# A diagonal state-space (S5) mixer on 32-column tiles of the array, with its short convolution as Toeplitz products read back from memory, inside a two-block network kernel

## The chip, the cores and the metric

One core of one Trainium2 chip runs one program. The metric is device time in microseconds (us), the median of several executions. TensorE is called PE, VectorE DVE, ScalarE ACT, GpSimd POOL; SP issues most transfers (DMAs).

## What is computed

The reference runs two blocks over 256 tokens of width 1024: an attention and expert block, then a block of two layers with four feed-forward networks (FFN 0 to 3), an S5 mixer between FFN 0 and 1, and an attention mixer. The change concerns the S5 mixer and FFN 0 ahead of it:

```python
u = (h @ w_in)                      # 256 x 1024, 64 groups of 16 channels
def step(carry, u_c):               # per chunk of time, per group: 64 complex states
    bu = einsum('bcgn,gpn->bcgp', u_c, bb)
    pr, pi, sr, si = lax.associative_scan(combine, (lam_re_b, lam_im_b, bu_re, bu_im), axis=1)
    ...
    y = einsum('bcgp,gnp->bcgn', st_re, c_re) - einsum('bcgp,gnp->bcgn', st_im, c_im)
y = y + d_skip * u
g = gelu(y)
g = g * sigmoid(g @ w_glu)
out = g @ w_out
```

## The kernel before

Everything is f32; matrix products split each factor into a rounded part and a rest (`wh`, `wl` of the weights, `xh`, `xl` of the activations) and add three products. Weights come in units of 512 KB in the order of use (`Stream`): SP loads `raw`, ACT rounds it to `wh` (L74), DVE subtracts to get `wl` (L75). FFN 0 has eight `raw` buffers, the mixer four, and two pairs `wh`, `wl`. A scheduler orders the instructions of each engine. Inside `manual_schedule`, PE and DVE follow the program text.

The mixer cuts the 256 tokens into 32 chunks of 8. Its parts, by the names in the code:

- `u_tile(f)`, f = 0 to 7: 24 products (L317 to L319, `s5ups`) and a scaling on DVE into `uT` (L1170).
- the gather: `uT` is written to `u_dram`, and after f = 3 and f = 7 read back in another layout as `us` (8 transfers of 512 runs of 128 bytes each).
- `contribution(hf)`, two halves: 64 narrow products (`s5eps`, 128 instructions, since an f32 product is two passes) give what each chunk adds to the states; ACT copies it to `s5e`.
- `chunks(hf)`: the recurrence over the chunks on DVE, in two blocks of 16 chunks side by side, then a correction of the second block. The two halves run by turns where both can.
- `taps(f)`: the part of y from inside a chunk, 8 products over weights that POOL and ACT spread by `tap_weights` (`s5kb`).
- `spread` and `states_out(qt)`: the states are put on a block diagonal (`s5sbd`), multiplied (`s5sps`), and go through `y_dram` to `yt` in four quarters.
- the sum, GELU, split, and the GLU: eight tiles of 24 products (`s5gps`) with a sigmoid each; then the output projection.

The part between the last u_tile and the GLU stands in this order in the text:

```python
contribution(0); taps(0); taps(1); run(45)
contribution(1); run(99, 24); spread(0); run(0, 99); spread(1)
taps(2) ... taps(5); states_out(0); taps(6); states_out(1); states_in(0)
taps(7); states_out(2); states_in(1); states_out(3); states_in(2); states_in(3)
```

Of the kernel before, what the change touches and what calls it, by code (L numbers as in the profile page):

```python
# [21 lines left out]
P = 128  # L22
D = 1024
S = 256
# [103 lines left out]
class Net:  # L128
# [4 lines left out]
    def __init__(self, ctx, tc, i, out, tap=None):  # L133
# [18 lines left out]
        self.v_order = [*range(self.NLO, P), *range(self.NLO)]  # L152
        self.ada_late = list(range(5, 5 + 8 * 5, 5))
# [158 lines left out]
    def mode_a(self, ps, w, xh, xl):  # L312

        wh, wl = w
        for k in range(KT):
# [564 lines left out]
    def ffn(self, l, last_deep=None, out=None):  # L880
        nc, tc = self.nc, self.tc
        with tc.tile_pool(name=f"ffn{l}", bufs=2) as fp:
# [5 lines left out]
            prev = row = None  # L888
            for c in range(NFF):
                if c == last_deep:  # L890
                    self.stream.shallow()
# [66 lines left out]
    def s5_prep(self, lo, hi):  # L958
# [169 lines left out]
        self.s5 = (lam, cw, me, kr, grp, pr, pi)  # L1128

    def s5_mixer(self):  # L1130
        nc, tc, i = self.nc, self.tc, self.i
        Q = 32
        lam, cw, me, kr, grp, pr, pi = self.s5
        with ExitStack() as st:
            wp = st.enter_context(tc.tile_pool(name="s5w", bufs=1))
            dp = st.enter_context(tc.tile_pool(name="s5d", bufs=1, space=bass.MemoryType.DRAM))
            u_dram = dp.tile([64, 16, 8, Q], F32, name="u_dram")
            y_dram = dp.tile([64, 16, 8, Q], F32, name="y_dram")
            xh, xl = self.gained(self.cols[:, self.MIX_G : self.MIX_G + KT])
            rx = self.rstd()  # L1140
            row = None
            l8 = wp.tile([P, 2, 2, Q], F32, name="s5l8")
# [4 lines left out]
            kbs = {}  # L1147

            uT = wp.tile([P, KT, 8, Q], F32, tag="sA", name="s5uT")
            us = wp.tile([P, 64, Q], F32, tag="sB", name="s5us")  # L1150
            def tap_weights(f):
                kb = wp.tile([P, 8, 8, 16], F32, tag="s5kb", name="s5kb", bufs=5)
                k = kr[:, f].rearrange("p (k n) -> p k n", n=16)
                if f % 2:
                    for g in range(8):
                        nc.scalar.activation(kb[:, :, g], k, AF.Copy, scale=grp[:, g : g + 1])
                else:
                    nc.gpsimd.tensor_mul(kb, k.unsqueeze(2).to_broadcast([P, 8, 8, 16]),
                                         grp[:, 0:8].unsqueeze(1).unsqueeze(3).to_broadcast([P, 8, 8, 16]))
                kbs[f] = kb  # L1160

            for f in (0, 2):
                tap_weights(f)
            def u_tile(f):
                nonlocal row
                ps = self.pm.tile([P, S], F32, tag="m", name="s5ups")
                self.mode_a(ps, self.stream.next(), xh, xl)
                if row is None:
                    row = self.rstd_row(wp, rx)
                nc.vector.tensor_mul(uT[:, f], ps.rearrange("p (c s) -> p s c", s=8),  # L1170
                                     row.rearrange("p (c s) -> p s c", s=8))
                nc.sync.dma_start(u_dram[8 * f : 8 * f + 8].rearrange("g n s c -> (g n) (s c)"),
                                  uT[:, f].rearrange("p s c -> p (s c)"))
                if f % 4 == 3:
                    gs = slice(8 * f - 24, 8 * f + 8)
                    for s in range(8):
                        nc.sync.dma_start(us[16 * s : 16 * s + 16, gs], u_dram[gs, :, s].rearrange("g n c -> n g c"))

            yc = wp.tile([P, KT, S], F32, name="s5yc")
# [3 lines left out]

            def taps(f):

                kb = kbs.pop(f)
                ps = self.pm.tile([P, S], F32, tag="m", name="s5yps")
                for k in range(8):
                    nc.tensor.matmul(ps[:, k * Q :], kb[:, k].rearrange("p a b -> p (a b)"),
                                     uT[:, f, 0 : 8 - k].rearrange("p s c -> p (s c)"), start=(k == 0), stop=(k == 7))  # L1190
                nc.scalar.activation(yc[:, f], ps, AF.Copy)

            def contribution(hf):

                for b in range(2):
                    ps = self.pa.tile([P, 2, 8, Q], F32, tag=f"acc{2 * hf + b}", name="s5eps")
                    for q8 in range(8):
                        q = 16 * hf + 8 * b + q8
                        for half in range(2):
                            hs = slice(64 * half, 64 * half + 64)  # L1200
                            for r in range(2):
                                nc.tensor.matmul(ps[hs, r, q8], me[q // 8][:, q % 8, r, hs], us[:, 2 * q + half], start=True, stop=True,
                                                 tile_position=(0, 64 * half))
                    nc.scalar.activation(ee[hf][:, :, :, 8 * b : 8 * b + 8].rearrange("p c r q -> p r q c"), ps, AF.Copy)

            def chunks(hf):
# [3 lines left out]
                s4 = ss[hf].rearrange("p (b c) r q -> p b c r q", b=2)  # L1210
                e4 = ee[hf].rearrange("p (b c) r q -> p b c r q", b=2)
                bl = lambda a: a.unsqueeze(1).to_broadcast([P, 2, 2, 16])
                yield v.memset(s4[:, :, 0], 0.0)
                for c in range(16):
                    n = 2 if c < 15 else 1
                    t = wp.tile([P, 2, 2, 2, 16], F32, tag=f"s5t{hf}", name="s5t")
                    t0, t1 = t[:, 0, :n], t[:, 1, :n]
                    if c < 15:
                        yield v.tensor_mul(t0, bl(l8[:, 0, :, qs]), s4[:, :, c])
                        yield v.tensor_mul(t1, bl(l8[:, 1, :, qs]), s4[:, :, c, ::-1])  # L1220
                        yield v.tensor_add(t0, t0, e4[:, :, c])
                        yield v.tensor_add(s4[:, :, c + 1], t0, t1)
                    else:
                        t0, t1, end = t0[:, 0], t1[:, 0], s4[:, 1, 0]
                        yield v.tensor_mul(t0, l8[:, 0, :, qs], s4[:, 0, c])
                        yield v.tensor_mul(t1, l8[:, 1, :, qs], s4[:, 0, c, ::-1])
                        yield v.tensor_add(t0, t0, e4[:, 0, c])
                        yield v.tensor_add(end, t0, t1)
                sh = [P, 15, 2, 16]
                x = wp.tile([P, 2, 15, 2, 16], F32, tag="sB", name="s5x")  # L1230
                x0, x1 = x[:, 0], x[:, 1]
                yield v.tensor_mul(x0, pr[:, :, qs].unsqueeze(2).to_broadcast(sh), end.unsqueeze(1).to_broadcast(sh))
                yield v.tensor_mul(x1, pi[:, :, :, qs], end[:, ::-1].unsqueeze(1).to_broadcast(sh))
                yield v.tensor_add(s4[:, 1, 1:], s4[:, 1, 1:], x0)
                yield v.tensor_add(s4[:, 1, 1:], s4[:, 1, 1:], x1)

            yt = None
            sbd = []
            for hf in range(2):
                sb = self.xt_pool.tile([P, 2, 16, 2, Q], F32, tag=("xh", "xl")[hf], name="s5sbd")  # L1240
                nc.gpsimd.memset(sb, 0.0)
                sbd.append(sb)

            def spread(hf):
                for half in range(2):
                    hs = slice(64 * half, 64 * half + 64)
                    src = ss[hf][hs].rearrange("p c r q -> p r q c")
                    if hf and half:
                        nc.vector.tensor_copy(sbd[hf][hs, :, :, half], src)
                    else:  # L1250
                        nc.scalar.activation(sbd[hf][hs, :, :, half], src, AF.Copy)

            ys = []

            def states_out(qt):

                ps = self.pa.tile([P, 8, 2, Q], F32, tag=f"acc{qt}", name="s5sps")
                for j in range(8):
                    for r in range(2):
                        nc.tensor.matmul(ps[:, j], cw[qt][:, r, j, 1:9].rearrange("p a b -> p (a b)"),  # L1260
                                         sbd[qt // 2][:, r, 8 * (qt % 2) + j], start=(r == 0), stop=(r == 1))
                if qt % 2 == 0:
                    ys.append(wp.tile([P, 2, 8, 2, Q], F32, tag=f"sE{qt // 2}", name="s5ys"))
                yb = ys[qt // 2][:, qt % 2]
                nc.scalar.activation(yb, ps, AF.Copy)
                for s in range(8):
                    q = nc.sync if s < 5 else nc.gpsimd
                    q.dma_start(y_dram[16 * qt : 16 * qt + 16, :, s].rearrange("g n c -> n g c"),
                                yb[16 * s : 16 * s + 16].rearrange("p q h c -> p (q h) c"))

            def states_in(qt):
                nc.sync.dma_start(yt[:, 2 * qt : 2 * qt + 2],
                                  y_dram[16 * qt : 16 * qt + 16].rearrange("(f g) n s c -> (g n) f (s c)", f=2))
# [3 lines left out]
            def run(n0, n1=0):  # L1277

                while n0 > 0 or n1 > 0:
                    if n0 > 0:  # L1280
                        next(rec0, None)
                    if n1 > 0:
                        next(rec1, None)
# [332 lines left out]
```

## Time and profile before

| what | value |
| --- | --- |
| median of 3 runs (lowest to highest) | 2130.15 us (2126.07 to 2134.4) |
| the profiled execution: time, span of its core | 2132.57 us, 2130.8 us |
| mean granted clock of PE, share of full speed | 0.981 |
| busy: PE, DVE, ACT, POOL | 94%, 74%, 50%, 25% |
| mean DMA rate | 178 GB/s |

A busy PE is one with an instruction in its pipeline, so 94% is not 94% of its peak. Shares are over the whole span; the mixer is some 147 us of it and has its own limits.

### The profile page before, as it was taken

How to read it: one execution, taken by the hardware profiler on the slowest of the kernel's cores; microseconds unless marked ns; L12 is line 12 of the kernel's file. 1: busy time of each engine (PE TensorE's matmuls, PEld its weight loads, DVE VectorE, ACT ScalarE, POOL GpSimd, SP SyncE). 2: the span in 40 equal slices, each digit the busy share in tenths (PEclk: the TensorE clock that was granted, in tenths of full speed). 3: DMA queues.
4: the chain of work that ended last, by engine and by line, in shares of the span. 5: the costliest groups of instructions: out<-in, count | busy, mean ns of one | idle time of the engine just before them, and what ended most of it. 6: DMA issues, size and time to landing. Idle time of an engine off the chain costs nothing. (4 is left out here: it accounts for less than half of the span.)

```text
span 2130.8 us, 33013 instructions
## 1 busy us (share of the span) xinstructions
PE 2010.9 (94%) x11862; PEld 1742.7 (82%) x11862; DVE 1572.3 (74%) x2984; ACT 1071.8 (50%) x1785; POOL 540.9 (25%) x548
## 2 busy tenths in 40 slices
PE   6888899999999899999999997889999999899999
PEld 4667899999999677788878887878887888677887
DVE  7987489887889666998866667476667666776666
ACT  5663544443444444545555544455555555555554
POOL 2342003036999332000031112101111111210111
PEclk9999999999999999999999999899999999999999
DMA  9763355554444777555555536355554555444552
GB/s 340 252 223 109 119 186 171 179 173 153 159 149 152 259 249 243 174 182 180 186 175 189 188 130 148 81 178 175 188 189 161 188 187 188 144 141 143 189 189 97
DMA packets 129557, 378.54 MB, mean 178 GB/s; under 512 B 26897, under 2 KB 41281, under 8 KB 129266
## 3 DMA queue, kind: packets, MB, share of 16 engines
q1 hardware_dynamic: 128160, 372.71, 52.5%
q0 software_dynamic: 1232, 3.73, 0.6%
q8 instruction: 93, 1.52, 0.3%
q14 instruction: 70, 0.57, 0.1%
q10 hardware_dynamic: 2, 0.00, 0.0%
HBM read 366.95 MB, written 9.44 MB: 177 GB/s over the span
## 5 line engine op out<-in xcount | busy, mean ns | idle before, releaser
L75 DVE TENSOR_TENSOR wl<-raw,wh 128x1024 fp32r<-128x1024 f32 (+1 forms) x595 | 761.4, 1282 | 366.8 <-ACT wh L74 363.2
L74 ACT ACTIVATE wh<-raw 128x1024 fp32r<-128x1024 f32 (+1 forms) x628 | 662.3, 1056 | 564.5 <-issue 317.1
L906 POOL TENSOR_TENSOR sgl<-sgl,rrow 128x256 f32<-128x256 f32 x88 | 126.2, 1434 | 719.7 <-ACT sgl L905 719.7
L317 PE MATMUL ups<-xh,wh 128*128 128x256 f32 x1024 | 294.1, 287 | 0.3 <-ACT act_lo L761 0.3
L319 PE MATMUL ups<-xh,wl 128*128 128x256 f32 x1024 | 290.5, 284 | 0.0
L318 PE MATMUL ups<-xl,wh 128*128 128x256 f32 x1024 | 290.3, 284 | 0.0
L327 PE MATMUL gps<-xx,wh 128*128 128x512 f32 x704 | 256.2, 401 | 6.6 <-DVE xx L306 6.6
L327 PE MATMUL upps<-xx,wh 128*128 128x512 f32 x704 | 251.8, 396 | 0.0
L335 PE MATMUL acc<-wh,gl 128*128 128x512 f32 x512 | 203.1, 399 | 8.1 <-DVE gl L250 8.1
L333 PE MATMUL acc<-wh,gh 128*128 128x512 f32 x512 | 203.6, 399 | 3.0 <-ACT gh L249 2.8
L685 POOL TENSOR_SCALAR ob<-iota,idxT 128x128 f32<-128x128 f32 x256 | 194.8, 781 | 36.0 <-PE ups L319 32.3
L328 PE MATMUL gps<-xx,wl 128*128 128x256 f32 x704 | 199.5, 283 | 0.6 <-DVE wl L75 0.6
L328 PE MATMUL upps<-xx,wl 128*128 128x256 f32 x704 | 198.4, 282 | 0.0
L317 PEld LDWEIGHTS ups<-xh,wh 128*128 128x128 f32 x1024 | 194.6, 190 | 0.8 <-ACT act_lo L761 0.7
L318 PEld LDWEIGHTS ups<-xl,wh 128*128 128x128 f32 x1024 | 194.6, 190 | 0.1
L319 PEld LDWEIGHTS ups<-xh,wl 128*128 128x128 f32 x1024 | 194.5, 190 | 0.1
L327 PEld LDWEIGHTS gps<-xx,wh 128*128 128x128 f32 x704 | 134.1, 190 | 38.6 <-DVE xx L306 7.8
L327 PEld LDWEIGHTS upps<-xx,wh 128*128 128x128 f32 x704 | 132.2, 188 | 31.2
L334 PE MATMUL acc<-wl,gh 128*128 128x512 f32 x380 | 151.3, 398 | 0.8 <-DVE wl L75 0.8
L333 PE MATMUL acc<-wh,hh 128*128 128x512 f32 x352 | 139.2, 396 | 6.7 <-ACT hh L249 6.5
L328 PEld LDWEIGHTS gps<-xx,wl 128*128 128x128 f32 x704 | 134.5, 191 | 4.5 <-DVE wl L75 0.9
L334 PE MATMUL acc<-wl,hh 128*128 128x512 f32 x352 | 137.9, 392 | 0.0
(403 smaller groups left out, 3779.6 us busy)
## 6 DMA issues: line engine op xcount, KB each, us to landing
raw<-peer_u SPq DMA_DIRECT2D x128, 512.0 KB, 3.3
raw<-peer_v SPq DMA_DIRECT2D x128, 512.0 KB, 3.4
raw<-ffn_gate SPq DMA_DIRECT2D x88, 512.0 KB, 3.6
raw<-ffn_up SPq DMA_DIRECT2D x88, 512.0 KB, 3.3
raw<-ffn_down SPq DMA_DIRECT2D x88, 512.0 KB, 3.4
raw<-w_ada SPq DMA_DIRECT2D x48, 512.0 KB, 5.6
raw<-w_in SPq DMA_DIRECT2D x24, 512.0 KB, 4.8
raw<-moba_w_qkv SPq DMA_DIRECT2D x24, 512.0 KB, 3.5
```

What stands on the lines that cost most here:

```text
L74: nc.scalar.activation(h[:, :n], raw[:, :n], AF.Copy)
L75: nc.vector.tensor_sub(lo[:, :n], raw[:, :n], h[:, :n].bitcast(F32))
L317: self.nc.tensor.matmul(ps, wh[:, s], xh[:, k], start=(k == 0), stop=False)
L318: self.nc.tensor.matmul(ps, wh[:, s], xl[:, k], start=False, stop=False)
L319: self.nc.tensor.matmul(ps, wl[:, s], xh[:, k], start=False, stop=(k == KT - 1))
L327: self.nc.tensor.matmul(ps, wh[:, s], xx[:, k], start=(k == 0), stop=False)
L328: self.nc.tensor.matmul(ps[:, 0], wl[:, s], xx[:, k, 0], start=False, stop=(k == KT - 1))
L333: mm(acc, lh, wh, start=start, stop=False)
L334: mm(acc, lh, wl, start=False, stop=False)
L335: mm(acc, ll, wh, start=False, stop=stop)
L685: nc.gpsimd.tensor_scalar(b, iota, idx[:, 1, n : n + 1], None, ALU.is_equal)
L906: nc.gpsimd.tensor_mul(sg, sg, row)
```

## The change

Four things change together. First, `u_tile` gets its weight columns in another order, so `uT` can be gathered from SBUF to SBUF with runs of 128, 384 or 512 bytes, without `u_dram`, in three pieces (f 0 to 3, 4 to 6, 7; of the last piece ACT issues half). Second, the taps become a Toeplitz matrix of 128 x 128 per group. FFN 0 writes it to DRAM (`toeplitz_out`: per f one transfer of zeros and eight of 16 rows of blocks), and the mixer reads half of it (2 MB) at a time into `s5tt`. Third, `taps` and `states_out` use 32 columns of the array per product (`tile_position`), with chunks in the rows of the result and both added in the same PSUM bank; no block diagonal, no `y_dram`: DVE transposes in blocks of 32 instead. Fourth, the recurrence runs in four blocks of 8 chunks, a sweep over the block ends and a correction, first half 0, then half 1.

```diff
+    def toeplitz_out(self, zero):
+        nc, kr = self.nc, self.s5[-1]
+        nc.gpsimd.memset(zero, 0.0)
+        for f in range(KT):
+            nc.sync.dma_start(self.toep[:, f].rearrange("p g k -> p (g k)"), zero)
+            for s in range(8):
+                nc.sync.dma_start(self.toep[16 * s : 16 * s + 16, f, :, 16 * s :].rearrange("n g k -> g n k"),
+                                    kr[:, f, : P - 16 * s])
...
             for c in range(NFF):
+                if 1 < c < NFF - 2:
+                    next(beside, None)
+                    next(beside, None)
...
+            def load_taps(hf):
+                toeplitz[hf] = wp.tile([P, 4, 8, P], F32, tag="s5tt", name="s5tt")
+                for f in range(4):
+                    nc.sync.dma_start(toeplitz[hf][:, f], self.toep[:, 4 * hf + f])
...
-            for f in (0, 2):
-                tap_weights(f)
+            pw = wp.tile([P, 2, 2, 8, 2, 16], F32, name="s5pw")
+            for hf in range(2):
+                qs = slice(16 * hf, 16 * hf + 16)
+                for r in range(2):
+                    nc.gpsimd.tensor_copy(pw[:, hf, 0, :, r], pr[:, :8, qs])
+                    nc.gpsimd.tensor_copy(pw[:, hf, 1, :, r], pi[:, :8, r, qs])
...
+            def gather(f0, f1):
+                for s in range(8):
+                    q = nc.scalar if f1 == KT and s % 2 else nc.sync
+                    q.dma_start(us[16 * s : 16 * s + 16, :, f0:f1].rearrange("p g f c -> p g (f c)"),
+                                uT[:, s, f0:f1].rearrange("p f c -> p (f c)"))
...
+                    for f in range(4):
+                        for j in range(4):
+                            nc.tensor.matmul(ps[32 * j : 32 * j + 32, f], us[:, 2 * j + half, 4 * hf + f],
+                                             toeplitz[hf][:, f, 2 * j + half], start=(f == 0), stop=False,
+                                             tile_position=(0, 32 * j))
...
+                                nc.tensor.matmul(yps[hf, half][32 * j : 32 * j + 32, f], ss[hf][hs, :, r, q % 16],
+                                                 cw[q // 8][hs, r, q % 8, 1:9].rearrange("p a b -> p (a b)"),
+                                                 start=False, stop=(f == 3 and r == 1), tile_position=(64 * half, 32 * j))
...
+                    nc.vector.transpose(yt[:, fs].rearrange("p f t -> p (f t)"),
+                                        yg[:, 8 * f : 8 * f + 16].rearrange("p a b c -> p (a b c)"))
+                    self.split(gh[:, fs], gl[:, fs], yt[:, fs])
```

The new order in the text, from u_tile 4 on:

```python
u_tile(4); u_tile(5); contribution(0); run(rec0, 1); run(rec1, 1); run(rec0, 8)
u_tile(6); gather(4, 7); run(rec0, 8); u_tile(7); gather(7, KT); taps(0); load_taps(1)
run(rec0, 99); contribution(1); taps(1); units = [stream.next()]; run(rec1, 20)
states_out(0); run(rec1, 99); states_out(1); units.append(stream.next())
# GLU: products 0 to 3 of its first two tiles, then products 4 to 7
```

On SP, where the mixer's transfers begin, stood before (`u_dram` is the written copy of `uT`, `s5us` the gathered one):

```order
L61 DMA raw<-s_w_in 128x1024 x7
L1172 DMA u_dram<-s5uT 128x256 x2
L61 DMA raw<-s_w_in 128x1024
L1172 DMA u_dram<-s5uT 128x256
L61 DMA raw<-s_w_glu 128x1024
L1172 DMA u_dram<-s5uT 128x256
L61 DMA raw<-s_w_glu 128x1024
L1177 DMA s5us<-u_dram 16x32x32 x8
```

and in the same place now:

```order
L61 DMA raw<-s_w_in 128x1024 x5
L1165 DMA s5tt<-toep_dram 128x1024 x3
L61 DMA raw<-s_w_in 128x1024
L1165 DMA s5tt<-toep_dram 128x1024
L61 DMA raw<-s_w_in 128x1024 x2
L61 DMA raw<-s_w_glu 128x1024
L1195 DMA s5us<-s5uT 16x8x128 x8
L61 DMA raw<-s_w_glu 128x1024 x3
L1195 DMA s5us<-s5uT 16x8x96 x8
L1195 DMA s5us<-s5uT 16x8x32 x4
L1165 DMA s5tt<-toep_dram 128x1024 x4
```

The write to `u_dram` is gone, the first half of the matrices is loaded ahead of the gathers, and the second half stands behind all of them.

On PE, from the last u_tile to the GLU, stood before (`s5eps` the contribution, `s5yps` the taps, `s5sps` the states, `s5gps` the GLU):

```order
L319 MATMUL s5ups<-xh,wl 128x256
L1202 MATMUL s5eps<-s5us,act_lo 64x32 x64
L1189 MATMUL s5yps<-s5uT,s5kb 128x256
...
L1202 MATMUL s5eps<-s5us,act_lo 64x32 x64
L1189 MATMUL s5yps<-s5uT,s5kb 128x256
...
L1260 MATMUL s5sps<-s5sbd,act_lo 128x64 x16
...
L1260 MATMUL s5sps<-s5sbd,act_lo 128x64 x32
L317 MATMUL s5gps<-xh,wh 128x256 x2
```

and now:

```order
L1211 MATMUL s5eps<-s5us,act_lo 64x32 x64
L319 MATMUL s5ups<-xh,wh 128x256
...
L1258 MATMUL s5yps<-s5tt,s5us 32x128 x32
L1211 MATMUL s5eps<-s5us,act_lo 64x32 x64
L1258 MATMUL s5yps<-s5tt,s5us 32x128 x32
L1270 MATMUL s5yps<-act_lo,s5s 32x128 x128
L319 MATMUL s5gps<-xh,wh 128x256
```

The first contribution moved ahead of u_tiles 6 and 7, and taps and states became 64 and 128 narrow products.

On DVE, at the end of the second half's recurrence, stood before (`s5s` the states, `xl` the rest of the GLU's input):

```order
L1234 TENSOR_TENSOR s5s<-s5s,s5x 128x480
L1235 TENSOR_TENSOR s5s<-s5s,s5x 128x480
L1249 COPY s5sbd<-s5s 64x32x32
L1325 TENSOR_TENSOR s5yt<-s5yt,s5yc 128x256 x2
L250 TENSOR_TENSOR xl<-s5yt,xh 128x256 x2
```

and now, in the middle of that recurrence (`s5t` a step's temporary, `s5yg` half 0 after the GELU):

```order
L1230 TENSOR_TENSOR s5s<-s5t 128x4x32
L1279 STREAM_TRANSPOSE s5yt<-s5yg 128x512
L252 TENSOR_TENSOR xl<-s5yt,xh 128x512
L1279 STREAM_TRANSPOSE s5yt<-s5yg 128x512
L252 TENSOR_TENSOR xl<-s5yt,xh 128x512
L1227 TENSOR_TENSOR s5t<-s5l_13576,s5s 128x128
```

The transposes of half 0 moved ahead of the last three of the eight steps of half 1, which are queued behind them.

## Rows read from the trace of the kernel before

**Rows 1.** View of stretches: busy time of each engine, clock, DMA share, GB/s.

```profile
core 0: us, PE busy (x) PEld busy (x) DVE busy (x) ACT busy (x) POOL busy (x), PEclk, DMA share, GB/s
1106.00:1283.50 177.50, 174.65 (x910) 148.44 (x909) 114.85 (x170) 89.50 (x148) 31.69 (x22) 1.00 0.51 170
...
1317.00:1376.00 59.00, 46.07 (x513) 44.88 (x512) 31.48 (x143) 23.25 (x41) 12.78 (x15) 0.91 0.34 74
```

**Rows 2.** Timeline of PE: start, duration, line, tile, count, [idle before, releaser].

```profile
1318.15 3.93 PE L1202 MATMUL s5eps<-s5us,act_lo 128*64 128x32 f32 x128 [1.13 <-DMA u_dram<-s5uT]
...
1331.98 5.36 PE L1202 MATMUL s5eps<-s5us,act_lo 128*64 128x32 f32 x128 [5.18 <-DMA s5us<-u_dram]
```

**Rows 3.** The GLU's tile: duration min/median/max, first and last start.

```profile
L319 PE MATMUL s5gps<-xh,wl x64: 274/281/420, 1376.9 to 1405.7; 128*128 128x256 f32 x64
```

**Rows 4.** Timeline of DVE at the last split ahead of the GLU.

```profile
1383.57 0.76 DVE L250 TENSOR_TENSOR xl<-s5yt,xh 128x256 fp32r<-128x256 f32 x2 [0.79 <-ACT xh L249]
```

**Rows 5.** Timeline of DVE: u_tiles 3 and 4, and a subtraction between.

```profile
1305.67 0.67 DVE L1170 TENSOR_TENSOR s5uT<-s5ups,rrow 128x256 f32<-128x256 f32 x1 [0.64 <-PE s5ups L319]
1306.65 1.23 DVE L75 TENSOR_TENSOR wl<-raw,wh 128x1024 fp32r<-128x1024 f32 x1 [0.30 <-ACT wh L74]
1308.52 0.67 DVE L1170 TENSOR_TENSOR s5uT<-s5ups,rrow 128x256 f32<-128x256 f32 x1 [0.65 <-PE s5ups L319]
```

**Rows 6.** Timeline of SP's queue: time taken to issue.

```profile
1306.37 0.32 SPq L1172 DMA_DIRECT2D u_dram<-s5uT  x1
...
1308.85 4.49 SPq L1177 DMA_DIRECT2D s5us<-u_dram  x8
```

**Rows 7.** View of DMAs, 1283 to 1400: KB each, median us to landing.

```profile
raw<-s_w_glu SPq DMA_DIRECT2D x8, 512.0 KB, 4.1
...
u_dram<-s5uT SPq DMA_DIRECT2D x8, 128.0 KB, 3.1
s5us<-u_dram SPq DMA_DIRECT2D x16, 64.0 KB, 4.7
...
y_dram<-s5ys SPq DMA_DIRECT2D x20, 32.0 KB, 2.0
```

**Rows 8.** Timeline of DVE: recurrence, 64, 480 and 32 elements per row.

```profile
1329.15 0.22 DVE L1222 TENSOR_TENSOR s5s<-s5t 128x64 f32<-128x64 f32 x1
...
1329.94 0.22 DVE L1222 TENSOR_TENSOR s5s<-s5t 128x64 f32<-128x64 f32 x1
...
1343.08 0.66 DVE L1232 TENSOR_TENSOR s5x<-act_lo,s5s 128x480 f32<-128x480 f32 x1
...
1353.83 0.19 DVE L1228 TENSOR_TENSOR s5s<-s5t 128x32 f32<-128x32 f32 x1
```

**Rows 9.** Timeline of ACT: two evictions of 128x512 from PSUM.

```profile
1322.12 1.06 ACT L1204 ACTIVATE s5e<-s5eps 128x512 f32<-128x512 f32 x1 [0.79 <-PE s5eps L1202]
...
1355.21 0.60 ACT L1265 ACTIVATE s5ys<-s5sps 128x512 f32<-128x512 f32 x1 [4.90 <-PE s5sps L1260]
```

**Rows 10.** Line L1108, 32-column products in the mixer's preparation.

```profile
L1108 PE MATMUL tps<-act_lo,gate_hi x128: 272/273/298, 1084.9 to 1088.4; 128*32 128x128 f32 x128
```

**Rows 11.** Timelines of POOL and DVE at the start, POOL's groups by form.

```profile
1283.81 5.75 POOL L1158 TENSOR_TENSOR s5kb<-act_lo 128x1024 f32<-128x1024 f32 x3 [4.67 <-PE acc L335]
...
1287.70 2.95 DVE L75 TENSOR_TENSOR wl<-raw,wh 128x1024 fp32r<-128x1024 f32 x1
...
L922 POOL TENSOR_TENSOR act_lo<-act_lo 128x128 f32<-128x128 f32 x1 | 0.4, 445 | 0.0
```

**Rows 12.** FFN 0: one row of its waits, SP's timeline, one of its DMAs.

```profile
ACT wh L74 <- DMA raw<-ffn_gate: 1.4, 1, 1.4
...
1233.86 0.33 SPq L61 DMA_DIRECT2D raw<-ffn_gate  x1
...
1242.27 0.33 SPq L61 DMA_DIRECT2D raw<-ffn_gate  x1
...
raw<-ffn_gate SPq DMA_DIRECT2D x17, 512.0 KB, 4.3
```

More of the change, by code (lines that the diff above doesn't have):

```diff
@@ L310, in gained, with mode_a @@
         return xh, xl
-    def mode_a(self, ps, w, xh, xl):
+    def mode_a(self, ps, w, xh, xl, ks=range(KT)):
         wh, wl = w
-        for k in range(KT):
+        for k in ks:
             s = slice(k * P, k * P + P)
@@ L1146, in s5_mixer @@
             nc.vector.tensor_copy(l8[:, 1, 1], lam[:, 1, 8])
[L1147 to L1160, printed above, removed]
-            for f in (0, 2):
-                tap_weights(f)
+            pw = wp.tile([P, 2, 2, 8, 2, 16], F32, name="s5pw")
[4 more added lines that the diff above has]
+                    nc.gpsimd.tensor_copy(pw[:, hf, 1, :, r], pi[:, :8, r, qs])
+            uT = wp.tile([P, 8, KT, Q], F32, tag="sA", name="s5uT")
+            us = wp.tile([P, 8, KT, Q], F32, tag="sB", name="s5us")
             def u_tile(f):
@@ L1229, in chunks @@
[L1229 to L1244, printed above, removed]
-                for half in range(2):
[L1246 to L1251, printed above, removed]
@@ L1286, in s5_mixer @@
-            for f in range(6):
+                    yield v.tensor_mul(t0, bl(l8[:, 0, :, qs]), s4[:, :n, c])
+                    yield v.tensor_mul(t1, bl(l8[:, 1, :, qs]), s4[:, :n, c, ::-1])
+                    yield v.tensor_add(t0, t0, e4[:, :n, c])
+                    yield v.tensor_add(s4[:, :, c + 1] if c < 7 else s4[:, 1:, 0], t0, t1)
+                sw = wp.tile([P, 3, 2, 16], F32, tag=f"s5sw{hf}", name="s5sw")
+                t = wp.tile([P, 2, 2, 16], F32, tag=f"s5u{hf}", name="s5u")
@@ new lines, in chunks, with taps @@
+                yield v.tensor_add(x[:, 0], x[:, 0], x[:, 1])
+                yield v.tensor_add(flat[:, 1:, 1:], flat[:, 1:, 1:], x[:, 0])
+            yps = {}
+            def taps(hf):
+                for half in range(2):
+                    ps = yps[hf, half] = self.pa.tile([P, 4, P], F32, tag=f"acc{2 * hf + half}", name="s5yps")
+                    for f in range(4):
[3 more added lines that the diff above has]
+                                             tile_position=(0, 32 * j))
@@ L1287, in s5_mixer, with run @@
+            rec0, rec1 = chunks(0), chunks(1)
+            def run(rec, n):
+                for _ in range(n):
+                    next(rec, None)
+            for f in range(4):
                 u_tile(f)
-                if f in (1, 3):
-                    tap_weights(f)
-            for f in range(4, KT):
-                tap_weights(f)
+            gather(0, 4)
+            load_taps(0)
             in_order = ExitStack()
             in_order.enter_context(tc.manual_schedule(engines={mybir.EngineType.PE, mybir.EngineType.DVE}))
+            u_tile(4)
@@ L1294, in s5_mixer @@
+            u_tile(5)
+            contribution(0)
+            run(rec0, 1)
+            run(rec1, 1)
+            run(rec0, 8)
             u_tile(6)
+            gather(4, 7)
+            run(rec0, 8)
             u_tile(7)
-            contribution(0)
+            gather(7, KT)
             taps(0)
+            load_taps(1)
+            run(rec0, 99)
+            contribution(1)
             taps(1)
-            run(45)
-            contribution(1)
-            run(99, 24)
-            spread(0)
@@ L1317, in s5_mixer @@
-            states_out(3)
-            states_in(2)
-            states_in(3)
-            in_order.close()
-            self.tap("s5yc", yc)
-            gh, gl = self.xt_tiles()
-            for f in range(KT):
-                nc.vector.tensor_add(yt[:, f], yt[:, f], yc[:, f])
-                nc.scalar.activation(yt[:, f], yt[:, f], AF.Gelu_apprx_tanh)
-                self.split(gh[:, f], gl[:, f], yt[:, f])
+            units.append(self.stream.next())
             oh = wp.tile([P, KT, S], F32R, tag="sA", name="s5oh")
@@ L1329, in s5_mixer @@
             ol = wp.tile([P, KT, S], F32R, tag="sS", name="s5ol")
-            for f in range(KT):
-                ps = self.pm.tile([P, S], F32, tag="m", name="s5gps")
-                self.mode_a(ps, self.stream.next(), gh, gl)
+            first = [(self.pm.tile([P, S], F32, tag="m", name="s5gps"), w) for w in units]
+            for ks in (range(4), range(4, KT)):
+                for ps, w in first:
+                    self.mode_a(ps, w, gh, gl, ks)
+            in_order.close()
+            for f in range(KT):
+                if f < 2:
+                    ps = first[f][0]
+                else:
+                    ps = self.pm.tile([P, S], F32, tag="m", name="s5gps")
+                    self.mode_a(ps, self.stream.next(), gh, gl)
```

124 lines of the change are left out of this document (49 added, 75 removed).

## The prediction

> **What bounds the kernel now.** I read the stretches first, then PE's timeline in the mixer, then what PE waits for. FFN 0 runs at full clock with PE hardly idle [rows 1]: there only lateness of weights could cost time, nothing can be gained. The 59 us between the last u_tile (1317) and the GLU (1376) are different: PE counts 46.07 us busy, the granted clock averages 0.91 (so part of the stretch is at the lower of the two levels, 1.2 and not 2.4 GHz), DVE is busy for half, DMA for a third [rows 1]. No engine bounds it; a chain of hand-overs does. PE waits for the gather before both contributions [rows 2], later for states, `y_dram` and the split, and the GLU starts at 1376 and ends at about 1406.0 [rows 3]. So the question is how long the new chain is, link by link, from the last instruction that both kernels have at the same time: the scaling of u_tile 3, which ends at 1306.34 [rows 5]. From there I carry times on the clock of the trace of before.
>
> **The change part by part.** *Gather of f 0 to 3.* Before, the written copy had to land before the reads were issued, at 1308.85 [rows 6], and PE began the first contribution at 1318.15, after u_tile 7 [rows 2]. Now SP issues eight transfers at once. One issue costs 0.32 (large) to 0.56 (4.49 / 8) [rows 6]; I take 0.45, so the last leaves at 1309.9. Landing took 2.0 us for 32 KB, 3.1 for 128 KB in large runs, 4.7 for 64 KB in 128-byte runs [rows 7]; with 512-byte runs I take 3.1: 1313.0. The contribution takes 3.9 [rows 2], to 1316.9, and its ACT copy 1.06 [rows 9]: 1318.0.
>
> *Recurrence of half 0.* A step of four instructions on 64 elements took 0.79 (1329.15 to 1329.94) [rows 8]. Between 64 and 480 elements an instruction grows by 0.44 us / 416, or 0.067 per 64 [rows 8]; four of them on 128 elements make a step of 1.06. Two steps (the first two instructions of the first are done early) end at 1319.7. Then follow in DVE's order `wl` (1.23), the scaling of u_tile 6 (0.67), two steps, `wl`, the scaling of u_tile 7 [rows 5]: 1325.6. PE's two u_tiles take 2.85 each (1308.52 less 1305.67) [rows 5] and u_tile 7 waits for the first of these `wl`; both fit. Before, u_tile 7 was through when PE went on at 1318.15 [rows 2], so the change first loses some 7 us here, with four of the eight steps done. Four more steps end at 1329.8. The sweep has ten instructions and a last copy on 32 elements, six of them waiting for the one before (0.19 plus a hand-over, 0.22 [rows 8]), the others at about half: 2.0. The correction has four on 672 elements (0.66 + 0.20 each [rows 8]): 3.4. Half 0 is ready at 1335.2; a `wl` makes it 1336.5.
>
> *Half 1 up to its states.* The gather of f 7: four issues per queue (1.8) and a landing of 2.5 (16 KB, nearest the 32 KB row; ends 2.0 and 4.7): 1329.9. PE has idled, so I take the 5.36 us of the second contribution before, not 3.9 [rows 2]: 1335.3, with its copy 1336.3, just ahead of DVE.
>
> *Matrices.* The first 2 MB go out near 1283 and stand there long before use. The second half waits for the first taps and stands behind the gathers: last issue 1329.2, landing 4.1 [rows 7], 1333.3. It hides under the contribution that ends at 1335.3. If its four transfers run no faster than FFN 0's mean rate, 170 GB/s [rows 1], 2 MB take 12 us and it lands near 1340: 5 us on the path. I take the first, since the bus is otherwise nearly idle there (0.34) [rows 1], and keep 5 for the range.
>
> *Narrow products.* The same kind already runs: 128 instructions with 32 columns and 128 elements from 1084.9 to 1088.4, so 27 ns each, although one lasts 273 [rows 10]: several run side by side. Second taps, 64 instructions: 1.7, to 1337.0. States of half 0, 128 instructions: 3.5, to 1340.5. The states use 64 rows, which no row shows; side by side in both row halves they could take half (1.7). If no tile ran beside another, each would cost four times as much, 109 ns, and the 128 would take 14: the upper end. I take 27 ns, the nearest row. The Trainium skill, "TensorEngine Tiling (Array Packing)", Tiling Modes, counts eight independent 64x32 tiles against four of 128x32; by that the states would take half, and the sum would be 3.5 us less. No run here shows it yet.
>
> *Out of half 0.* Two GELUs at 0.60 [rows 9]: 1341.8. DVE has finished five steps of half 1 at 1336.5 + 5.3 = 1341.8 as well. A block transpose is not in the trace. I price it like other DVE work on 512 elements, 0.7 (ends 0.35 and 1.4), then ACT's rounding 0.65, the subtraction 0.76 [rows 4], and hand-overs: 2.2, twice, 4.4, to 1346.2. The last three steps of half 1 (3.2) and its tail (5.4) stand behind that: 1354.8.
>
> *Out of half 1.* States: PE has idled for 14 us, so between 3.5 and 7, 5.1: 1359.9. GELU and transposes 5.7: last `xl` at 1365.6. Before, the last `xl` ended at 1384.33 [rows 4] and the GLU at 1406.0, 21.7 later [rows 3]; the first two tiles are then half done in both. GLU end 1387.3, against 1406.0: **18.7 us saved**.
>
> *Start of the mixer.* Before, POOL multiplied `s5kb` for 5.75 us and a `wl` beside it took 2.95 and not 1.23 [rows 11, 5]. Now POOL makes eight copies, at most 0.45 each [rows 11], so 3.6. I credit 1.0 of the 1.7 (ends 0 and 3).
>
> *FFN 0.* SP issues 72 more transfers. A loop takes 8.4 us (1242.27 less 1233.86) with three weight units [rows 12], and 12 to 13 loops take all 72, so 6 per loop: 6 x 0.56 + 3 x 0.33 = 4.4 us of 8.4. The units land in 4.3 us and ACT waited for one only once, 1.4 us [rows 12]; with eight buffers a unit may be several us late. The cover is this lead. I take 0. If each extra transfer held SP for over (8.4 - 1.0) / 6 = 1.2 us, SP would set the pace; that is the end I keep (up to +5 for a partial one).
>
> **Sum.** 2132.57 - 18.7 - 1.0 = 2112.9 against the profiled execution, whose time is 2.4 above the median shown. Against the median: **2110.5 us**.
>
> **Rivals.**
>
> *A. The chain as computed*, 0.66.
>
> *B. Less gain: the hand-overs between DVE and PE stretch.* Late matrices (+5), narrow products at the lower clock throughout (+3.5), transposes at 1.4 (+2.8): about 2121. For it: the granted clock of 0.91 and the 5.36 against 3.93 [rows 1, 2]; against: each is an end. 0.13. If the 64-row products do not overlap at all, each half costs 10.6 more, 21 in all, and the gain is gone: 2132. Against: [rows 10]. That is in this 0.13 with about 0.03.
>
> *C. More gain.* The eight tiles really overlap twice as well (-3.5), transposes take 0.35 (-1.4), the start gains 3 (-2): 2103 or less. 0.12.
>
> *D. Slower: FFN 0's SP queue clogs.* If each of the 64 strided writes held SP until it landed, at 3.1 us each [rows 7], that is 198 us in the 105 of 12.5 loops, 93 too much; the lead of eight units covers some 22 (8 x 2.8), so FFN 0 would end 71 late: 2184. At 2.0 us each it is 128, and the lead just covers the 23 too much. It turns the sign from 2.3 us per write on: (105 + 22 + 20) / 64. The Trainium skill, "DMA: Bandwidth & Descriptors", Specifications, says transfers below 512 bytes are read, modified and written back, which speaks against the 56 writes with shorter runs. The trace is milder: 32 KB in 128-byte runs to DRAM landed in 2.0 us [rows 7]. 0.05. Something between, a few us late, stays within A and B. The last 0.04 is a wait that I don't see and that takes the gain or more.
>
> **Numbers.** All bounds in one direction: 2.1 (gathers) + 3.4 (tiles) + 1.4 + 2 = 9 less, 2101; or 5 + 3.5 + 2.8 + 5 (gathers' landing, twice) + 5 (FFN 0) = 21 more, 2132. Not all come together: 2102 to 2121 holds A, half of C and most of B. About 0.5% (10.7 us, 2119.5) is what a measurement of this kernel can tell from no change: the three runs differ by 0.4%. Faster: A, C and a part of B, 0.84; same: 0.09; slower: D and the rest, 0.07.
>
> **What would show it.** Right: first contribution near 1313 on this clock, u_tile 7 scaled about 8 us later than before, second taps near 1335, GLU end near 1387 (the start of the mixer at the same time), 27 ns per narrow product. Wrong: FFN 0 longer than before or ACT waiting for `raw` there; second taps waiting for `s5tt`; 128 narrow products taking over 7 us; a transpose far over 0.7; five steps of half 1 not done when the GELU is.

## The result and the profile after

The changed kernel takes 2112.68 us (median of 4 runs, 2109.44 to 2114.71) against 2128.63 for the kernel before (4 runs beside it, 2126.07 to 2134.4): ratio 0.992, 95% interval 0.9895 to 0.9945. That is 0.8% faster, inside the predicted range and 2.2 us above the predicted time. The profiled execution takes 2114.71 us with a span of 2112.9, so 17.9 us less than that of before.

Where the 17.9 us lie is read from two marks that both kernels have: the first `sgl` of FFN 0 and its first residual addition into `x_sb`. Timelines of POOL and DVE after the change:

```profile
1104.54 0.73 POOL L912 TENSOR_TENSOR sgl<-sgl,rrow 128x256 f32<-128x256 f32 x1 [18.24 <-ACT sgl L911]
...
1280.12 1.29 DVE L878 SCALAR_TENSOR_TENSOR x_sb<-acc,x_sb 128x512 f32<-128x512 f32 x2 [0.70 <-PE acc L337]
```

Before, the marks stood at 1106.99 and 1282.6. So 2.45 us were there ahead of FFN 0, in code that the change does not touch (in the runs below that first `sgl` lies anywhere from 1095.8 to 1107.3); FFN 0 takes 175.6 us in both; the rest is the mixer, less 0.6 us lost behind it. I call **M** the time from that residual addition to the start of the last `s5gps` product. It was 123.1 us (1405.7 less 1282.6 [rows 3]) and is 107.1 (1387.21 less 1280.12): 16.0 us. M leaves out what varies ahead of FFN 0. In two runs below whose mixer is that of the change it came out at 107.15 and 108.56, so differences under 1.5 us say nothing unless an earlier mark shows them too. The medians differ by as much (2128.63 less 2112.68 is 15.95).

Stretches after (columns as in [rows 1]):

```profile
1106.00:1281.00 175.00, 173.27 (x902) 147.53 (x903) 113.64 (x168) 88.00 (x145) 30.96 (x21) 1.00 0.63 203
1283.00:1315.00 32.00, 28.20 (x305) 26.77 (x306) 18.66 (x46) 13.25 (x21) 0.32 (x2) 0.95 0.52 179
1315.00:1360.00 45.00, 19.81 (x541) 17.52 (x539) 30.98 (x97) 7.89 (x9) 0.00 (x0) 0.75 0.29 95
```

FFN 0 carries the writes (203 GB/s, 170 before [rows 1]) and PE stays busy at full clock. Between 1315 and 1360 PE is busy for 19.81 of 45 us at a mean of 0.75, a mix of the two levels: still a chain of hand-overs. Its links, on PE, then SP (the stretch of time from the first issue of a row to the end of the last; below it, one issue in ns, min/median/max, and two of SP's waits: total us, times, longest), ACT and DVE:

```profile
1307.05 5.46 PE L1211 MATMUL s5eps<-s5us,act_lo 128*64 128x32 f32 x128 [2.32 <-DMA s5us<-s5uT]
...
1326.76 5.81 PE L1211 MATMUL s5eps<-s5us,act_lo 128*64 128x32 f32 x128 [5.45 <-DMA s5us<-s5uT]
...
1336.54 1.30 PE L1258 MATMUL s5yps<-s5tt,s5us 128*32 128x128 f32 x40 [1.10 <-DMA s5tt<-toep_dram]
1337.77 1.87 PE L1270 MATMUL s5yps<-act_lo,s5s 64*32 64x128 f32 x103
1341.01 0.70 PE L1270 MATMUL s5yps<-act_lo,s5s 64*32 64x128 f32 x25 [1.37 <-issue]
...
1356.54 3.70 PE L1270 MATMUL s5yps<-act_lo,s5s 64*32 64x128 f32 x128 [14.84 <-DVE s5s L1248]
```

```profile
1299.78 5.13 SPq L1195 DMA_DIRECT2D s5us<-s5uT  x8
...
1317.07 10.45 SPq L1195 DMA_DIRECT2D s5us<-s5uT  x12
...
1327.62 2.81 SPq L1165 DMA_DIRECT2D s5tt<-toep_dram  x4
```

```profile
L1195 SPq DMA_DIRECT2D s5us<-s5uT x20: 547/597/804, 1299.8 to 1326.9; - x20
...
SPq L1195 <- DMA raw<-s_w_glu: 1.4, 1, 1.4
SPq L1195 <- DMA s5us<-s5uT: 1.4, 1, 1.4
```

```profile
1341.66 1.28 ACT L1275 ACT_TABLE_LOAD   x1 [8.02 <-PE s5yps L1270]
```

```profile
1344.07 0.71 DVE L1279 STREAM_TRANSPOSE s5yt<-s5yg 128x512 f32<-128x512 f32 x1 [5.55 <-ACT s5yg L1275]
```

An issue of a gather takes 0.60 us (median). The first eight follow one another, 5.13 us in all; the row of twelve takes 10.45 us, because SP also waits in it, 1.4 us each, for an earlier load and for an earlier gather to land. So the 0.87 us each (10.45 / 12) of an expectation below is not the price of an issue. The second taps wait for `s5tt`; the states of half 0 pause for 1.37 us (1339.64 to 1341.01), for which the profile names no releaser; the GELU's table is loaded in line; DVE idles 5.55 us for the GELU with three steps of half 1 behind it; PE then waits 14.84 us for half 1's states.

### The profile page after: what moved, and what is told of

The parts are those of the page before. It is cut to its first block, busy times and chain, and to the rows that moved or that the text cites. A ratio compares the mean times of both kernels' runs of the same rounds, so it can differ in the third digit from the quotient of the medians.

```text
span 2112.9 us, 33176 instructions
## 1 busy us (share of the span) xinstructions
PE 1987.7 (94%) x11990; PEld 1718.4 (81%) x11990; DVE 1563.6 (74%) x2933; ACT 1051.4 (50%) x1730; POOL 524.4 (25%) x539
## 3 DMA queue, kind: packets, MB, share of 16 engines
q8 instruction: 94, 1.54, 0.3%
```

## Experiments

Theory: that chain sets M, and each of these links is on it. Rival: another thing does (the form of the recurrence, its turns, the writes in FFN 0), and the links hide behind it. u_tile 3 is given as the time of its scaling after the residual addition. The last column is how long contribution(0) took: the granted clock in it varies from run to run, and that alone can move M by some 1.5 us either way. All experiments but the two "together" without filler are one execution each.

| run | M us | u_tile 3 | FFN 0 us | contribution(0) us |
|---|---|---|---|---|
| before | 123.1 | 23.1 | 175.6 | 3.9 |
| after | 107.1 | 19.0 | 175.6 | 5.5 |
| issues split | 102.2 | 19.0 | 175.5 | 3.9 |
| first taps early | 105.3 | 19.9 | 175.5 | 5.5 |
| half 1 first | 97.7 | 19.0 | 175.6 | 5.5 |
| two blocks | 107.6 | 19.0 | 175.5 | 5.5 |
| turns | 106.1 | 18.9 | 175.6 | 7.1 |
| POOL's work back | 108.9 | 21.3 | 175.6 | 5.5 |
| ACT's work back | 108.7 | 18.9 | 175.5 | 6.4 |
| writes twice | 107.2 | 19.0 | 203.4 | 5.5 |
| strided writes twice | 108.6 | 19.0 | 193.0 | 5.5 |
| together, load on POOL | 97.5 | 19.0 | 175.6 | 3.9 |
| the same with filler | 98.9 | 19.8 | 175.5 | 5.5 |
| together, load on SP | 94.8 | 19.0 | 175.6 | 5.5 |

**Issues split.**
```diff
-q = nc.scalar if f1 == KT and s % 2 else nc.sync
+q = nc.scalar if s % 2 else nc.sync
```


> All gathers alternate between SP and ACT, not only that of f 7. M is the time from the first residual addition of FFN 0 to the start of the last s5gps product: 123.1 us in the trace of before, 107.1 after the change. Theory (the issues on SP set both gathers: 8 took 5.13 us and 12 took 10.45, 0.64 and 0.87 each): contribution(0) starts some 2 us earlier (PE idled 2.32 ahead of it), contribution(1) some 3 us earlier, the second half of the matrices goes out 3 us earlier, M 104 to 104.5. Rival (landing, not issuing, sets them; the two queues share what carries the data): the last transfer lands when it did, M 106.6 to 107.6.

M 102.2, a larger gain than the theory had. View of the tile `s5us` in this run (count; issue in ns min/median/max; first and last start):

```profile
L1195 SPq DMA_DIRECT2D s5us<-s5uT x8: 547/594/638, 1316.3 to 1322.9; - x8
L1195 ACTq DMA_DIRECT2D s5us<-s5uT x8: 554/624/892, 1316.3 to 1322.5; - x8
```
Each issue still takes 0.6 us, but two queues do them: the last is done at 1323.5, 41.5 us after the residual addition (1281.98 here), and not 47.4 (1327.52 less 1280.12). Some 1.5 of M's 4.9 us are the clock: contribution(0) ran at 1.00 here and took 3.9 us in place of 5.46. The rest, 3.4, is the split. Landing has a share, as the rival said: 2.8 of the 10.45 us after the change are SP's two waits for landings, and here PE waits 1.80 us within contribution(1) for the last transfer.

**First taps early.**
```diff
 contribution(0)
+taps(0)
+load_taps(1)
...
-taps(0)
-load_taps(1)
```


> The first taps stand right behind contribution(0), so the single buffer is free some 6 us earlier, and the second half of the matrices is issued ahead of the second gather. Theory (the second half of the matrices held the second taps for 1.52 + 1.10 us): no wait for s5tt is left, taps(1) follow contribution(1) directly, M 104.5 (2.6 less than 107.1). Rival (the wait only moves: the first taps, 1.95 us, now delay u_tile 6 and 7 and with them the second gather): contribution(1) starts 1 to 2 us later, M 106 to 107.

Both happened. The wait for `s5tt` is gone (contribution(1) ends, taps(1) follow at once), and u_tile 6 and contribution(1) come 2.3 and 2.2 us later, 0.9 of which u_tile 3 already had. M falls by 1.8, at the edge of what it can tell.

**Half 1 first.**
```diff
-run(rec1, 20)
+run(rec1, 99)
...
 states_out(0)
-run(rec1, 99)
 states_out(1)
```


> All eight steps and the tail of half 1's recurrence stand ahead of half 0's transposes on DVE. DVE idled 5.55 us for the GELU there. Theory (half 1's last three steps and tail, 8.4 us, were queued behind that wait and 4.1 us of transposes): half 1 is ready 9 us earlier, its states' products follow half 0's within a few us, last xl some 8.5 us earlier, M 98 to 99. Rival (the transposes of both halves, now back to back, and PE at the lower clock take it again): M 102 or more.

M 97.7, as the theory had it, a little better. Timelines of PE and of DVE in this run:

```profile
1342.58 3.71 PE L1270 MATMUL s5yps<-act_lo,s5s 64*32 64x128 f32 x128 [5.67 <-DVE s5s L1248]
```
```profile
1341.67 0.86 DVE L1248 TENSOR_TENSOR s5s<-s5s,s5x 128x672 f32<-128x672 f32 x1
1342.45 0.70 DVE L1279 STREAM_TRANSPOSE s5yt<-s5yg 128x512 f32<-128x512 f32 x1
```
PE waits 5.67 us for half 1's states and not 14.84. Half 0's transposes find the GELU long done.

**Two blocks.** The recurrence of before (16 steps on 64 elements, a correction of four on 480) replaces the body of `chunks`, in the order of the change.

> The recurrence of before (16 steps on 64 elements and a correction of four on 480) in the place of the new one (8 steps on 128 and a tail), still in sequence. Theory: 16 steps at 0.79 and a tail of 2.8 are 15.4 us a half against 13.9; half 0's share is hidden behind contribution(1), half 1's rest behind the transposes is 11 steps and the tail, 11.5 us in place of 8.4: M 110.2. Rival 1 (DVE waits for others there, the form of the recurrence is off the path): M 107.1. Rival 2 (both halves on the path, and hand-overs of the shorter instructions cost more): M 112 or more.

M 107.6: rival 1 by the number, but not for its reason. Behind the transposes half 1 does take longer, 11.1 us and not 8.4, as the theory said. What it missed is that the pieces ahead are shorter: two steps between u_tiles take 1.6 and not 2.1 us, so u_tile 7 is scaled 0.9 us sooner and half 0's GELU comes 2.1 us sooner (60.7 us after the residual addition, not 62.8).

**Turns.** contribution(1) goes ahead, and half 0's and half 1's instructions then alternate on DVE.
```diff
-run(rec0, 99)
 contribution(1)
+for _ in range(99):
+    run(rec0, 1)
+    run(rec1, 1)
...
-run(rec1, 20)
...
-run(rec1, 99)
```


> The recurrences take turns, as before the change: contribution(1) first, then instruction by instruction half 0's remaining four steps and tail beside half 1's. Theory (DVE's order decides, as in the run with half 1's recurrence first; half 0 then waits for contribution(1)'s copy, some 23 us of DVE work stands behind it, and both halves' products, GELU and transposes come together): half 1's states are ready at about the time they are in the change (76 us from the start of M), both transposes stand behind it; M 106 to 109, that is, turns against the change's order are worth nothing, but cost 9 to 11 us against half 1's recurrence first (97.7). Rival (turns fill the waits between dependent instructions, so 3 to 5 us less DVE time): M 102 to 104.

M 106.1, the theory's lower end. But contribution(0) took 7.05 us in this run, and u_tile 7 was scaled 2.2 us later than after the change. At the same clock turns might be some 3 us ahead of the change's order, in the rival's range; that is an estimate, and no run shows it. Where half 1's tail stands against half 0's transposes is worth 9.4 us (half 1 first).

**The start: POOL's work back, ACT's work back.**
```diff
+for f in (0, 2):
+    nc.gpsimd.tensor_mul(kb, ...)
```


> Two products of 128x1024 on POOL at the start of the mixer, as before the change, into a scratch buffer that nothing reads. Theory (POOL beside DVE slowed the first wl from 1.23 to 2.95 us and that held the first u_tiles): u_tile 3 is scaled 2 to 4 us later than the 16.1 us from the first residual addition that it takes in the change; M 109 to 111. Rival (ACT's 16 activations did it): u_tile 3 at the same place, M 107.1.

```diff
+if f in (1, 3):
+    for g in range(8):
+        nc.scalar.activation(kb[:, :, g], k, AF.Copy, scale=grp[:, g : g + 1])
```


> Sixteen ACT activations of 128x128 at the start of the mixer, as before the change, into a scratch buffer that nothing reads. Theory (POOL did it): ACT has room, u_tile 3 moves by less than 1 us, M 107 to 108. Rival (ACT rounds the weights and splits x there, and 16 more activations stand ahead of that): u_tile 3 later by 2 to 4 us, M 109 to 111. Both can hold in part; the two runs together should give back the 4.2 us that the start gained.

u_tile 3 starts at 19.0 us after the change; the 16.1 us in the first expectation is the start of u_tile 2. With ACT's work u_tile 3 does not move; M's 1.6 is the lower clock in contribution(0) (6.37 us in place of 5.46) and in u_tile 6, which is scaled 2.1 us later. With POOL's work, two products here and three before the change, u_tile 3 is 2.3 us late. Timelines of POOL and of DVE with POOL's work back:

```profile
1274.53 4.96 POOL L1184 TENSOR_TENSOR s5kb<-act_lo 128x1024 f32<-128x1024 f32 x2
```
```profile
1274.95 1.54 DVE L1171 TENSOR_SCALAR s5l<-act_lo 128x32 f32<-128x32 f32 x1
...
1276.49 1.21 DVE L75 TENSOR_TENSOR wl<-raw,wh 128x1024 fp32r<-128x1024 f32 x1
...
1278.41 1.09 DVE L275 TENSOR_TENSOR s<-ss 128x2 f32<-128x2 f32 x1
```
A `TENSOR_SCALAR` of 32 elements takes 1.54 us and a `TENSOR_TENSOR` of 2 elements 1.09; after the change, without POOL's products, they take 0.17 and 0.16. The two make the 2.3 us; DVE has no idle time between them. This time `wl` is not hit: POOL's products began later than before the change, after the `s5pw` copies, and `wl` fell ahead of the second one. The Trainium skill, "SBUF — State Buffer", Who interferes with whom, has GpSimd, and DVE where its instruction needs them, lock a shared pair of ports for a whole instruction, so that the second one blocks. The rows agree: the two DVE instructions end within 0.04 us of the end of a POOL product, and the POOL product that began just behind `wl` took 2.96 us and the other 1.93. The eight transposes named next took 1.94 us in this run too, but DVE did not wait for them.

Before the change the same is seen on two more DVE groups than the `wl` of [rows 11], first two lines; the last two are eight transposes on PE, before and after the change:

```profile
1284.95 0.92 DVE L1144 COPY s5l<-act_lo 128x32 f32<-128x32 f32 x2
1286.57 1.12 DVE L1145 TENSOR_SCALAR s5l<-act_lo 128x32 f32<-128x32 f32 x1
...
1291.24 1.91 PE L295 MATMUL xps<-ident,x_sb 128*128 128x128 f32 x8
...
1285.63 1.06 PE L297 MATMUL xps<-ident,x_sb 128*128 128x128 f32 x8
```
These three DVE groups make 3.2 of the 4.1 us that u_tile 3 gained. The remaining 0.9 goes with the transposes: the granted clock was 0.57 there (1290.5 to 1294.5), after PE had idled 3.5 us for the slow `wl`, and 1.00 after the change. In two runs without POOL's products (first taps early, and the one with filler below) they also took 1.91 us, and u_tile 3 was 0.9 us late.

**Writes twice, strided writes twice.** A second array in DRAM takes the same transfers: first zeros and strided pieces (144 in all), then the strided pieces alone (136).
```diff
+for toep in (self.toep, self.toep2):
     nc.sync.dma_start(toep[16 * s : 16 * s + 16, f, :, 16 * s :]..., kr[:, f, : P - 16 * s])
```


> FFN 0 writes the matrices twice, to two places: 144 transfers in the same loops, 12 a loop and not 6. FFN 0 from its first sgl to its first residual addition takes 175.6 us before and 175.55 after. Theory (the writes hold only SP, 0.60 to 0.72 each in the trace of after, and the weights have a lead): 12 at 0.63 and 3 weight units at 0.38 are 8.7 us of SP in a loop of 8.4, 4 us late after 12 loops, which the lead covers: 175.5 to 177. Rival (short writes are carried out by more than their bytes and eat the bandwidth of the weights): 180 or more, with ACT waiting for raw.

> FFN 0 writes the strided pieces twice (to two places), but fills only the first place with zeros: 136 transfers, as many waits for a zero fill as in the change. With everything twice FFN 0 took 203.4 us in place of 175.6; there SP waited 31.0 us in 14 waits for zero fills to land (5.8 in 4 after the change), with the weights' transfers queued behind. Theory (the waits for the zero fills did it): SP works 128 x 0.62 + 8 x 0.46 + 36 x 0.4 + 6 = 103 us in the 100 to 105 of the loops, and FFN 0 takes 175.5 to 179. Rival (the strided writes themselves do it, by issuing or by bandwidth): 190 or more.

My theory fell twice: 203.4 and 193.0 us. What SP waits for in FFN 0 (total us, times, longest), first with all written twice, then with the strided writes alone twice:

```profile
SPq L1146 <- DMA toep_dram<-zero: 31.0, 14, 6.9
```
```profile
SPq L1145 <- DMA toep_dram<-zero: 16.2, 6, 5.3
```
The waits for the zero fills do not explain the second run alone: it adds no zero fill, and they still grew from 5.8 us to 16.2. SP's own time does, roughly. With 0.62 a write, 0.46 a zero fill and 14 us for the weights, the second run has 128 x 0.62 + 4 + 14 + 16 = 113 and the first 79 + 7 + 14 + 31 = 131 in some 105 us of loops, so 8 and 26 too much, against 17.4 and 27.8 measured. The change has 40 + 4 + 14 + 6 = 64 of 105 and loses nothing. What the last 9 us of the second run are is open; the lead of the weights covered none of it, contrary to what I had assumed. The rivals had the size, but bandwidth is not seen to have run out: the 16 DMA engines were busy for 0.63 and 0.62 of FFN 0, as in the change (0.63).

**Together.** The split issues, half 1 first, and two smaller edits: the GELU's table loaded behind contribution(1) by a GELU of 128x1, and `load_taps(1)` issued by POOL.
```diff
+q = nc.gpsimd if hf else nc.sync
 for f in range(4):
-    nc.sync.dma_start(toeplitz[hf][:, f], self.toep[:, 4 * hf + f])
+    q.dma_start(toeplitz[hf][:, f], self.toep[:, 4 * hf + f])
```


> The gathers alternate between SP and ACT, half 1's recurrence stands ahead of half 0's transposes, the second half of the matrices is issued by POOL, and the GELU's table is loaded behind contribution(1)'s copy. Theory (from the copy of contribution(0) on DVE is then the one chain: half 0's rest, half 1's steps and tail without a wait, 13.7 us, then both transposes): e1's 4.9 and e3's 9.4 us add, less 1 to 2 since DVE no longer waits anywhere for what the table and the matrices gave; M 91.5 to 93.5, the time 15 us less than that of the change. Rival (the two share a wait, so their gains do not add; POOL's issues cost more than SP's): M 95 or more.

M 97.5, no better than half 1 first alone; 2105.44 us (ratio 0.986, 0.9826 to 0.9895). Timelines of POOL and of PE in it:

```profile
1322.21 2.17 POOL L1166 DMA_DIRECT2D s5tt<-toep_dram  x4 [36.14 <-DMA s5us<-s5uT]
```
```profile
1333.35 1.94 PE L1212 MATMUL s5eps<-s5us,act_lo 128*64 128x32 f32 x32 [7.23 <-DMA s5us<-s5uT]
```
The 2 MB leave POOL at 1322.2 to 1324.4, while SP and ACT issue the last gather up to 1325.2; it lands only near 1333.3, and PE waits 7.23 us for it. With the same gathers and the matrices behind them on SP (issues split), the last landing came by 1326.7, 3.2 us after the last issue was done. The Trainium skill, "DMA: Bandwidth & Descriptors", Queues, rings and completion order, has each DMA engine take the queues that have work in turn; that fits, though no run here shows the turns themselves.

The same with twenty products of 128x256 into an unused tile between `states_out(0)` and `states_out(1)`:

> As f1, and twenty products of 128x256 into an unused PSUM tile between the states' products of half 0 and half 1, so that TensorE works while it waits for DVE. They compute nothing that is used. Theory (PE comes to half 1's states at the lower clock since it idled: 3.70 us for 128 records, 29 ns each, against 18 at full clock): half 1's states take 2.4 us and the first GLU products start at full clock, M 1 to 2 less than f1. Rival 1 (the clock there follows something else): the granted clock in that stretch stays near 0.5, M as f1. Rival 2 (the fillers themselves run at the lower clock and are not done when the states are): M 1 to 8 more than f1.

```profile
1336.13 8.90 PE L1321 MATMUL warm<-s5tt 128*128 128x256 f32 x40
1345.74 2.25 PE L1271 MATMUL s5yps<-act_lo,s5s 64*32 64x128 f32 x128 [0.71 <-DVE s5s L1249]
```
Half 1's states take 2.25 us and not 3.71: the lower clock came from the idling. But from their start to the end of M it is 30.0 us (1375.78 less 1345.74) against 30.7 without filler: 0.6 us, since DVE's transposes of half 0 stand there anyway. One run shows this. M itself, 98.9, is higher because this run lost 0.9 at the start and 1.4 more by u_tile 7.

At last the matrices go back to SP, behind the gathers, with the other three edits kept and no filler:

> As f1, but SP issues the second half of the matrices behind the gathers again. In f1 POOL issued it at 1322.21, beside the gather of f 7, and the last transfers of that gather, issued by 1325.3, landed at 1333.3; with the gathers split and the matrices behind them on SP they had landed by 1326.7. Theory (2 MB that go out beside a small gather hold it back): contribution(1) ends some 8 us earlier than in f1 on the clock of M, DVE goes from half 0 to half 1 without a wait, M 92 to 94, which is e1's 4.9 us and e3's 9.4 us added, less at most 1. Rival (the gains of e1 and e3 do not add, whatever issues the matrices): M 96 or more.

2097.93 us (median of 5, 2094.09 to 2104.43; before 2132.37 beside it, 9 runs): ratio 0.9833, 95% interval 0.982 to 0.9847. M is 94.8, 0.8 above the theory's range and below the rival's. What DVE waits for from the first copy of `s5e` to the last split (total us, times, longest), after the change and then here:

```profile
DVE s5yt L1279 <- ACT s5yg L1275: 10.5, 2, 5.5
DVE s5t L1229 <- ACT s5e L1213: 9.7, 2, 7.6
DVE xl L252 <- ACT xh L251: 2.8, 4, 0.7
```
```profile
DVE s5t L1229 <- ACT s5e L1213: 6.8, 1, 6.8
DVE xl L252 <- ACT xh L251: 2.8, 4, 0.7
DVE s5yt L1279 <- ACT s5yg L1275: 0.9, 1, 0.9
```
The wait for half 1's copy is gone and those for the GELU fall from 10.5 to 0.9 us: from contribution(0)'s copy to the transposes DVE is the bound. The missing 2 us of the sum is contribution(0): it ran at 0.69 here and at 1.00 with the issues split, so that DVE began 2.0 us later.

No run takes the first three parts of the change (the gather within SBUF, the Toeplitz matrices, the narrow products) apart. Only the fourth was taken back by itself (two blocks, 0.5 us), so how the gain divides among the others is not shown.

## Why the prediction was right, point by point

- **Bound and chain: right; its size was not.** No engine bounds the mixer. The GLU ended at 1387.5, on the clock of before at 1394.1 (u_tile 3 ends 6.6 us earlier after the change) where 1387.3 was forecast: the chain gave 11.9 us of the 18.7.
- **Issues: mis-sized.** 0.45 us was taken and 0.60 measured; the row it came from issued other transfers [rows 6]. What cost more was SP's queue: four issues behind u_tile 7's scaling were counted, but on SP four of f 4 to 6 still stood ahead of them, with a wait of 1.4 us for a landing between. With the lower clock in contribution(0), contribution(1) began 3.5 us late. The split run shows that SP's row of issues, its waits included, holds it.
- **Second matrices: the step that failed.** "It hides under the contribution" was wrong; the taps waited 1.52 and 1.10 us, and their end was 7.4 us late, 3.6 of it from here (2.6 of waiting, the rest slower products). The loads stand behind the gathers' issues on SP and began at 1327.62; their buffer was free at 1321.3, when the first taps were done, so it was not the buffer. The run with the first taps early, which moves the loads ahead of these issues, removes the wait.
- **GELU's table: not in the sum.** 1.28 us in line. The two GELUs took 1.08 for 1.2. No run moves the table alone. The pause of 1.37 us in the states of half 0 was not in the sum either; its cause is not shown. A load on the DMA queue for instructions ended 1.4 us before the pause did, and 1.5 to 1.6 us before the like pauses in four of the runs (first taps early, half 1 first, two blocks, POOL's work back), which hints at code that came late.
- **Contributions: 3.9 and 5.36 forecast, 5.46 and 5.81 measured**, at a granted clock of 0.69 and 0.64 there.
- **Narrow products: between the two prices.** 27 ns from start to start was taken. The states' products follow one another in 16 ns at full clock ((1.87 - 0.27) / 102, since a single one lasts 0.27 us) and, with (3.70 - 0.41) / 127, in 26 after idling. The Trainium skill's count of eight tiles (TensorEngine Tiling (Array Packing), Tiling Modes) would have halved 27 to 13.5; at full clock the measured gain is two fifths, so the direction agrees and the size nearly does. The 18 and 29 ns in an expectation above spread the last product's duration over the others.
- **DVE's steps, tail, transposes: right.** A step of 1.06, as forecast; half 1's rest 8.4 for 8.6; a transpose 0.71 for 0.7, with rounding and split 4.1 a half for 4.4.
- **Start: under-sized, 1.0 for 4.2.** I counted only `wl`. In the trace of before two small DVE groups beside POOL's products were stretched as well, 0.92 for 0.36 and 1.12 for 0.17, which with `wl` (2.95 for 1.22) makes 3.2 of the 4.1 us at u_tile 3. The runs show that POOL does this and ACT does not; the other 0.9 goes with eight transposes at the lower clock.
- **FFN 0: right, 0.** At about twice the transfers SP's queue does clog, but not as rival D had it: a write held SP for some 0.6 us and not until it landed.

The bound was understood, but that the total came so close is luck, since errors cancelled: 6.8 us less from the chain, against 3.2 more from the start and 2.4 that lay ahead of FFN 0 in the profiled execution.

## What to carry to other kernels

Where a chain of hand-overs bounds a stage, price issues from rows of the same kind of transfer, and sum up the issuing queue: FFN 0 took 72 transfers for nothing and lost 17 to 28 us at twice as many. Then look what stands in order behind a waiting instruction: moving one call so that one half's recurrence does not queue behind the other's transposes gave 9.4 us, over half of what the whole change gave. Keep a large transfer behind the small one that the next step waits for, even where another queue is free to issue it: that order was worth 2.8 us of M here, with contribution(0) 1.5 us slower.

## Not expected of the hardware

- Issuing a transfer from SBUF into 16 partitions of SBUF holds the queue for 0.55 to 0.9 us on SP and on ACT alike.
- One POOL product stretched a DVE instruction of 32 elements from 0.17 to 1.54 us; the next one was held up itself, 2.96 for 1.93 us, behind a DVE instruction that came first.
- 2 MB issued beside a gather of 16 KB transfers put its landing off by some 5 us: the last came 8.1 us after the last issue was done, 3.2 without.
- The same contribution(0) took 3.9 to 7.1 us from run to run, by the granted clock: 1.00 in two runs of those after the change, 0.69 in most, 0.57 and 0.50 in one each. PE idled 1.2 to 2.3 us ahead of it; after the same 1.66 us it ran at 1.00 once (load on POOL) and at 0.69 once (load on SP).
